# Low parts of weights made by adding loads, and more row pairs in seven products, in the last feed-forward layer of a decoder trunk

## The chip, the cores and the metric

One core of one Trainium2 chip. The metric is the device time of one execution in microseconds (us), taken as the median of several runs: 2597.03 us for the kernel before (3 runs, 2595.98 to 2597.09).

## What is computed

A trunk of two layers over 256 tokens of width 2048. Layer 0 mixes tokens by multi-scale retention, layer 1 by a short gated convolution; each is followed by a SwiGLU feed-forward of inner width 5632. Every sub-layer has an RMS norm, a shift, scale and gate from a conditioning vector, and a residual add. The change touches only the last feed-forward:

```python
def swiglu(h, w_in, w_out):
    a, b = jnp.split(h @ w_in, 2, axis=-1)
    return (jax.nn.silu(a) * b) @ w_out

# per layer i, after its mixer
h = (rms_norm(x, norm2_g[i]) * (1.0 + sc2) + sh2).astype(x.dtype)
x = (x + g2 * swiglu(h, ffn_w_in[i], ffn_w_out[i])).astype(x.dtype)
# at the end
return rms_norm(x, final_g).astype(x.dtype)
```

All is in float32.

## The kernel before, in words

**Products from high and low parts.** TensorE (PE) multiplies in a shortened float format (fp32r). To keep precision, every operand is split: hi is the value cast to fp32r, lo is the value minus hi. A product then takes three matmuls: hi by hi, hi by lo, lo by hi (`thrice`, lines 457 to 462; L461 is the one that reads the weights' low part).

**Where weights come from.** All weights but those of the modulation lie in one array `w_all` of 456 blocks of 128 x 2048 floats (1 MB), in the order of use. `fetch` (L370) loads a block into a `raw` buffer (three of them), by the queue of SyncE (SP). `prepare` (L376) turns it into pieces: for a plain block two halves of 1024 columns, pieces 0 and 1. For each, ScalarE (ACT) casts the half to `hi` (L402), and VectorE (DVE) subtracts to `lo` (L405). `hi` and `lo` have four buffers each (`PART_BUFS`), so piece n can be written only when PE has done with piece n - 4. `take` (L410) hands the parts of a piece to PE and, when it begins a piece, prepares on so that in the last stage three pieces lie ahead (`ahead_now`). PE's instructions stay in the order of the program; those of the other engines are ordered by a scheduler, close to the program's order.

**The last stage.** The last feed-forward holds tokens on the rows: 256 tokens are two halves of 128. Weights are taken in blocks of two rows (of 128) by two columns (of 512). Plain (`Group`), such a block takes 8 products of 128 x 128 by 128 x 512, that is 24 matmuls; each piece of 1024 columns serves 12. In sevens (`Seven`, L142; `sevens`, L1222) the same block takes 7 products by the Strassen-Winograd scheme, with sums and differences of the four weight parts and of the four token parts: 21 matmuls. For its weights `prepare` makes four pieces, 2 to 5: VectorE makes a difference of 1024 columns (L391) and two of 512 (L395, L397), and the pieces have 1024, 1024, 1024 and 512 columns. Pieces 2 to 4 serve 6 matmuls each and piece 5 serves 3. The token sums are made once for each row pair: for the input rows by `made_in_sums` before the first group, for output rows by `turned` (L1323) just after the two rows exist, both through `tokens_sums_of` (L1138). After the last block in sevens of a group, `mixed_sums` (L1235) combines four banks on VectorE.

The input projection runs in groups of eight row pairs (0 to 7), four groups in part 0 and six in part 1; before, pairs 3 and 5 go in sevens (`IN_SEVEN`). A group's result passes through SiLU and product, and is turned (eight transposes, L1329) during the next group, when that reaches its third row pair (`TURNS_AT`). The output projection runs after each part, in two groups of 1024 columns: ten row pairs in part 0, twelve in part 1, of which the three pairs 2, 4, 6 go in sevens (`OUT_SEVEN`). In the last output group the last three pairs are taken by single columns, for the tail. The grouped part of the last stage is the last 124 of the 456 blocks; 32 of them are in sevens before.

Of the kernel before, what the change touches and what calls it, by code (L numbers as in the profile page):

```python
# [10 lines left out]
F32 = mybir.dt.float32  # L11
F32R = mybir.dt.float32r
I32 = mybir.dt.int32
AF = mybir.ActivationFunctionType
ALU = mybir.AluOpType
PSUM = bass.MemoryType.PSUM

P = 128
# [14 lines left out]
HALF = 1024  # L33
# [4 lines left out]
LEAD = 6  # L38
ROOTS_AT, SPREAD_AT = 1, 3
TAIL_ROWS = 6  # L40
IN_SEVEN, OUT_SEVEN, TURNS_AT, BESIDE_CB, BESIDE_SUMS = (3, 5), (2, 4, 6), 2, 40, 48
LAST_TILES = 20, 24
STORE_AT, LOAD_AT = 0, 2
LEAD_RET, LEAD_CONV, LEAD_FFN = 6, 4, 2
# [97 lines left out]
class Seven:  # L142
# [6 lines left out]
    n = 2 * DV // P  # L149
# [12 lines left out]
def in_pairs(cols, rows, sevens):  # L162

    return [Seven(cols, r) if i in sevens else Group(cols, DV, ks=r) for i, r in rows]
# [13 lines left out]
def last_out(part):  # L178

    first, n = part * LAST_TILES[0], LAST_TILES[part]  # L180
    order = list(range(n // 2))
    if not part:
        a, b = order[-2:]
        order = order[:5] + [a, order[6], b, order[5], order[7]]
    rows = [(i, [first + 2 * i, first + 2 * i + 1]) for i in order]
    out = []
    for c in range(0, D, 2 * DV):
        cols, rest = [c, c + DV], 0
        if part and c + 2 * DV == D:
            rest = TAIL_ROWS // 2  # L190
        out.append(in_pairs(cols, rows[: len(rows) - rest], OUT_SEVEN))
        if rest:
            out[-1] += [Group([col], DV, ks=[k for _, r in rows[-rest:] for k in r]) for col in cols]
    return out
# [62 lines left out]
def trunk(ctx: ExitStack, tc: tile.TileContext, x_in, c_in, pos_in, w_mod, cols_in, gain_in, tab_in, w_all, out):  # L257
    nc = tc.nc
# [11 lines left out]
    def tmp(tag, shape=(P, S), dtype=F32, pool=work, bufs=None):  # L270
        return pool.tile(list(shape), dtype, tag=tag, name=name(tag), bufs=bufs)
# [11 lines left out]
    cols = const.tile([P, n_cols], F32, tag="cols", name="cols")  # L283
# [78 lines left out]
    in_seven, n = set(), 0  # L362
    for g in groups:
        if isinstance(g, Seven):
            in_seven.add(n // CHUNK)
        n += g.n * P * len(g.ks)

    pieces = [(i, p) for i in range(w_all.shape[0]) for p in ((2, 3, 4, 5) if i in in_seven else (0, 1))]

    def fetch():  # L370
        raw = wpool.tile([P, CHUNK], F32, tag="raw", name=name("raw"), bufs=RAW_BUFS)
# [4 lines left out]
    def prepare(between=None):  # L376
        if prepared[0] == len(pieces):
            return
        _, piece = pieces[prepared[0]]
        prepared[0] += 1  # L380
        if piece in (0, 2):
            if not fetched:
                fetch()
            raws[:] = [fetched.pop(0)]
            while first <= units[0] < early and len(fetched) < RAW_BUFS - 1 and n_fetched[0] < w_all.shape[0]:
                fetch()
        whole = raws[0]
        b = [whole[:, i : i + DV] for i in range(0, CHUNK, DV)]
        raw = whole[:, :HALF] if piece in (0, 4) else whole[:, HALF:]
        if piece == 2:  # L390
            nc.vector.tensor_tensor(differences, whole[:, DV : 3 * DV], whole[:, : 2 * DV], op=ALU.subtract)  # L391
        elif piece == 3:
            raw = differences
        elif piece == 4:
            nc.vector.tensor_tensor(b[1], b[2], differences[:, :DV], op=ALU.subtract)  # L395
        elif piece == 5:
            nc.vector.tensor_tensor(b[3], b[3], b[1], op=ALU.subtract)  # L397
            raw = b[3]
        width = raw.shape[1]
        hi = wpool.tile([P, HALF], F32R, tag="hi", name=name("hi"))[:, :width]  # L400
        lo = wpool.tile([P, HALF], F32R, tag="lo", name=name("lo"))[:, :width]
        nc.scalar.copy(hi, raw)  # L402
        if between:
            between()
        nc.vector.tensor_tensor(lo, raw, hi.bitcast(F32), op=ALU.subtract)  # L405
        ready.append((hi, lo, width))

    prepared, ahead_now = [0], [AHEAD]
# [270 lines left out]
    with ExitStack() as inner:  # L679
# [64 lines left out]
        with tc.tile_pool(name="start", bufs=1) as sp:  # L744
# [132 lines left out]
            due, step = [], [0.0]  # L877
# [245 lines left out]
    def turn(t, c):  # L1123
# [8 lines left out]
    needed(1, GT2)  # L1132
    in_cb = const.tile([P, D], F32R, tag="cb", name="in_cb")
    tokens_sums = [
        v.rearrange("p (i n) -> p i n", i=2) for v in (in_cb[:, : 6 * P], in_cb[:, 6 * P : 12 * P])
    ] + [mpool.tile([P, 2, 3 * P], F32R, tag="sums_of_tokens", name="sums_of_tokens")]

    def tokens_sums_of(a11, a21, a12, a22, third, others):  # L1138

# [11 lines left out]
    def parts(both):  # L1151

        return [both[:, i, t * P : (t + 1) * P] for i in range(2) for t in range(2)]

    in_sums = {}

    def made_in_sums():

        tmp("beside_sums", (P, BESIDE_SUMS), bufs=1)
        for i in IN_SEVEN:  # L1160
            both = tmp("u512", (P, 2, S), pool=mpool, bufs=3)
            for n in range(2):
                k = 2 * i + n
                high, low = [h[k].bitcast(F32)[:, v, :] for v in range(2)]
                nc.vector.tensor_tensor(both[:, n, :], high, low, op=ALU.add)
            tag = "low" if in_sums else "u"
            in_sums[i] = [tmp(tag, (P, 2, P), F32R, bufs=3) for _ in range(3)]
            tokens_sums_of(*parts(both), h[2 * i][:, :, P:], in_sums[i])

    def three(v):  # L1170
        return [v[:, :, n * P : (n + 1) * P] for n in range(3)]

    turns = [lambda t=t, c=c: turn(t, c) for c in range(4) for t in range(2)]

# [136 lines left out]
    def last_input(groups, pairs, seven):  # L1311

        ours, extra = gathered(groups, h, 0, in_sums)
        for (t, j), pt in ours.items():
            nc.vector.tensor_tensor(extra[t, j], pt, extra[t, j], op=ALU.add)
        ms = []
        for t in range(2):
            m = extra[t, 0]
            nc.scalar.activation(m, m, AF.Silu)
            nc.vector.tensor_tensor(m, m, extra[t, 1], op=ALU.mult)  # L1320
            ms.append(m)

        def turned():  # L1323
            for n, (dst, of) in enumerate(zip(pairs, seven)):
                pt = bank()
                for i in range(2):
                    for t, m in enumerate(ms):
                        c = slice((2 * n + i) * P, (2 * n + i + 1) * P)
                        nc.tensor.transpose(pt[:, i, t * P : (t + 1) * P], m[:, c], ident)  # L1329
                if of is not None:  # L1330
                    both = tmp("u512", (P, 2, S), pool=mpool, bufs=3)
                    nc.scalar.copy(both, pt)
                nc.scalar.copy(dst[:, :, 0, :], pt)
                nc.vector.tensor_tensor(dst[:, :, 1, :], pt, dst[:, :, 0, :].bitcast(F32), op=ALU.subtract)
                if of is not None:
                    tokens_sums_of(*parts(both), dst[:, 0, :, P:], [of])

        waiting.append(turned)

    def last_output(part, c, groups, act, base):  # L1340

        final = part and c

        def beside(i):
            if not part and not c and i == STORE_AT:
                gate_stored()
            if not part and not c and i == LOAD_AT:
                spread()
            if part and not c and i == LOAD_AT:
                last_gain = hpool.tile([P, D], F32, tag="h", name="last_gain")  # L1350
                nc.sync.dma_start(last_gain, gain_in.broadcast_to([P, D]))
                gain_of.extend(at(last_gain, v) for v in range(4))

        def mixed(extra):
            for (t, j), v in extra.items():
                gated(t, c + j, v, 0)

        sums = {i: three(v) for i, v in zip(OUT_SEVEN, tokens_sums)}
        ours, extra = gathered(groups, act, base, sums, beside, mixed if final else None)
        if final:  # L1360
            return
        for (t, j), pt in ours.items():
            nc.vector.tensor_tensor(extra[t, j], pt, extra[t, j], op=ALU.add)
        for (t, j), v in extra.items():
            gated(t, c + j, v, MOD_PRIO)
            if part:
                xs, n = at(xt[t], c + j), c + j
                nc.scalar.activation(v, xs, AF.Square, accum_out=total[:, t, n : n + 1])
                nc.vector.tensor_tensor(xs, xs, gain_of[n], op=ALU.mult)
# [16 lines left out]
    for part in range(2):  # L1386
        n = LAST_TILES[part] // 2
        mid = mids(LAST_TILES[part]) if part else first_mid
        if not part:
            first_rows(mid[-2:])  # L1390
            made_in_sums()
            ahead_now[0] = AHEAD + 1
        for i, groups in enumerate(LAST_IN[part]):
            seven = [tokens_sums[OUT_SEVEN.index(q)] if q in OUT_SEVEN else None for q in (2 * i, 2 * i + 1)]
            last_input(groups, mid[2 * i : 2 * i + 2], seven)
        act = [mid[k // 2][:, k % 2] for k in range(2 * n)]
        for c, groups in enumerate(LAST_OUT[part]):
            last_output(part, 2 * c, groups, act, part * LAST_TILES[0])
# [37 lines left out]
```

## Time and profile before

| | |
|---|---|
| median of 3 runs | 2597.03 us |
| profiled execution, its own time | 2600.71 us |
| its span, first to last instruction | 2598.8 us |
| granted TensorE clock, mean | 0.999 |
| read from memory | 685.08 MB, 264 GB/s over the span |
| raw loads of `w_all` | 456 of 1024 KB, median 4.9 us from issue to landing |
| weight subtractions on VectorE (L405) | 944, 1129.9 us |
| weight casts on ScalarE (L402) | 944, 973.1 us |

How to read it: PE is TensorE's matmuls, PEld its weight loads, POOL is GpSimd, SP is SyncE. "busy" is the time in which an engine had an instruction running; matmuls are pipelined, so that two that follow each other overlap in the rows. In groups of instructions, `out<-in` names what is written and read, `xcount` is how often, then come the busy time and the mean of one in ns, and behind the second bar the engine's idle time ahead of these instructions and what ended it. "DMA share" is the mean busy share of the core's 16 DMA engines.

### The profile page before, as it was taken

Reading aid. Unit: us, or ns where it says so; the run is one execution under the profiler, and the core shown is the slowest. Engines: PE = TensorE matmul, PEld = TensorE weight load, DVE = VectorE, ACT = ScalarE, POOL = GpSimd, SP = SyncE. Lnnn points to the kernel's source line nnn. Section 1 sums busy time; section 2 is a strip of 40 time slices with the busy share of each in tenths; the row PEclk is TensorE's granted clock in tenths of the full one; section 3 lists DMA queues with packets and bytes.
Section 4 is the critical chain, followed back from the end, with each engine's and each line's share of the span. In section 5 each row is a group of like instructions: output and inputs, shape, how many; then the busy total and the mean of one; then the engine's idle time right before and its main releaser. Section 6 shows DMA issues by size and latency. Waiting matters only on the chain.

```text
span 2598.8 us, 36365 instructions
## 1 busy us (share of the span) xinstructions
PE 2567.0 (99%) x14211; PEld 2241.0 (86%) x14211; DVE 2157.4 (83%) x2702; ACT 1289.4 (50%) x1768; POOL 125.7 (5%) x232
## 2 busy tenths in 40 slices
PE   7999999999999999999999999999999999999998
PEld 6898889888889888888888898888998888888886
DVE  7988978887698887777777889988988888888877
ACT  5544543444456454334444454444565554555554
POOL 0000000110000000100001001000000000000000
PEclk9999999999999999999999999999999999999999
DMA  9975668877676888787778868877845565554653
GB/s 399 387 290 221 255 246 300 299 261 276 244 284 247 330 325 305 298 299 302 294 284 296 299 237 313 326 290 277 305 171 204 190 217 203 184 207 182 221 200 146
DMA packets 96686, 689.55 MB, mean 265 GB/s; under 512 B 10737, under 2 KB 12161, under 8 KB 13441
## 3 DMA queue, kind: packets, MB, share of 16 engines
q1 hardware_dynamic: 96514, 687.23, 71.1%
q8 instruction: 111, 1.82, 0.3%
q14 instruction: 61, 0.50, 0.1%
HBM read 685.08 MB, written 2.11 MB: 264 GB/s over the span
## 4 chain that ended last, share of the span: by engine, by line
PE 84%; DVE 7%; DMA 5%; issue 2%; ACT 1%; ACTq 0%; POOLq 0%; POOL 0%; DVEq 0%; SPq 0%
PE bank L447 25%; PE bank L450 14%; PE bank L461 12%; PE bank L460 12%; PE bank L462 12%; DMA raw<-w_all 4%; DVE lo L405 3%; DMA raw<-w_mod 2%; PE bank L496 2%; PE bank L495 1%; PE bank L494 1%; PE bank L627 1%; PE bank L629 1%; PE bank L628 1%; DVE raw L755 1%
## 5 line engine op out<-in xcount | busy, mean ns | idle before, releaser
L402 ACT CAST hi<-raw 128x1024 fp32r<-128x1024 f32 (+1 forms) x944 | 973.1, 1039 | 1037.0 <-PE bank L462 385.6
L405 DVE TENSOR_TENSOR lo<-raw,hi 128x1024 fp32r<-128x1024 f32 (+1 forms) x944 | 1129.9, 1203 | 347.4 <-ACT hi L402 340.0
L447 PE MATMUL bank<-h,hi 128*128 128x512 f32 x2016 | 699.2, 390 | 0.0
L450 PE MATMUL bank<-h,lo 128*128 128x256 f32 x2016 | 568.4, 282 | 0.0
L447 PEld LDWEIGHTS bank<-h,hi 128*128 128x128 f32 x2016 | 378.3, 188 | 79.2
L460 PE MATMUL bank<-hi,h 128*128 128x512 f32 x1072 | 420.1, 392 | 1.8 <-DVE rm L739 1.8
L461 PE MATMUL bank<-lo,h 128*128 128x512 f32 x1072 | 418.3, 390 | 0.7 <-DVE lo L405 0.7
L462 PE MATMUL bank<-hi,h 128*128 128x512 f32 x1072 | 417.6, 390 | 0.0
L318 DVE SCALAR_TENSOR_TENSOR raw<-raw,cb 128x2048 f32<-128x2048 f32 x160 | 365.6, 2285 | 23.2 <-DMA raw<-w_mod 22.9
L450 PEld LDWEIGHTS bank<-h,lo 128*128 128x128 f32 x2016 | 381.0, 189 | 0.0
L447 PE MATMUL bank<-mid,hi 128*128 128x512 f32 x922 | 319.8, 390 | 0.0
L450 PE MATMUL bank<-mid,lo 128*128 128x256 f32 x922 | 260.1, 282 | 0.4 <-DVE lo L405 0.4
L462 PEld LDWEIGHTS bank<-hi,h 128*128 128x128 f32 x1072 | 201.4, 188 | 42.6
L460 PEld LDWEIGHTS bank<-hi,h 128*128 128x128 f32 x1072 | 201.8, 188 | 41.8 <-DVE rm L739 2.4
L461 PEld LDWEIGHTS bank<-lo,h 128*128 128x128 f32 x1072 | 201.9, 188 | 39.9 <-DVE lo L405 1.1
L447 PEld LDWEIGHTS bank<-mid,hi 128*128 128x128 f32 x922 | 173.0, 188 | 36.2
L450 PEld LDWEIGHTS bank<-mid,lo 128*128 128x128 f32 x922 | 174.3, 189 | 0.7 <-DVE lo L405 0.7
L447 PE MATMUL bank<-rm,hi 128*128 128x512 f32 x496 | 172.6, 390 | 0.0
L496 PE MATMUL bank<-h,lo 128*128 128x256 f32 x512 | 146.2, 286 | 5.2 <-DVE lo L405 5.2
L494 PE MATMUL bank<-h,hi 128*128 128x256 f32 x512 | 145.6, 284 | 3.2 <-ACT h L783 3.2
L495 PE MATMUL bank<-h,hi 128*128 128x256 f32 x512 | 145.6, 284 | 0.7 <-DVE h L784 0.7
L450 PE MATMUL bank<-rm,lo 128*128 128x256 f32 x496 | 139.9, 282 | 0.0
(248 smaller groups left out, 3092.4 us busy)
## 6 DMA issues: line engine op xcount, KB each, us to landing
raw<-w_all SPq DMA_DIRECT2D x456, 1024.0 KB, 4.9
raw<-w_mod SPq DMA_DIRECT2D x192, 1024.0 KB, 5.3
x<-x_in SPq DMA_DIRECT2D x4, 512.0 KB, 5.5
out<-xt SPq DMA_DIRECT2D x4, 512.0 KB, 3.0
decay<-tab_in SPq DMA_DIRECT2D x8, 128.0 KB, 2.7
x<-gate_row SPq DMA_DIRECT2D x2, 512.0 KB, 4.4
last_gain<-gain_in SPq DMA_DIRECT2D x1, 1024.0 KB, 4.6
cols<-cols_in SPq DMA_DIRECT2D x1, 152.0 KB, 8.5
```

Source lines behind the costliest of these rows:

```text
L318: nc.vector.scalar_tensor_tensor(raw, raw, 1.0, cb, op0=ALU.mult, op1=ALU.mult, accum_out=total)
L402: nc.scalar.copy(hi, raw)
L405: nc.vector.tensor_tensor(lo, raw, hi.bitcast(F32), op=ALU.subtract)
L447: nc.tensor.matmul(pt, hi, h, start=fresh and k == g.ks[0], stop=False, skip_group_check=True)
L450: nc.tensor.matmul(pt[:, 1, :], lo, h[:, 0, :], start=False, stop=last and k == g.ks[-1], skip_group_check=True)
L460: nc.tensor.matmul(o, hi, w_hi, start=first, stop=False)
L461: nc.tensor.matmul(o, hi, w_lo, start=False, stop=False)
L462: nc.tensor.matmul(o, lo, w_hi, start=False, stop=last)
L494: nc.tensor.matmul(pt, hi, h[:, 0, :], start=first, stop=False, skip_group_check=True)
L495: nc.tensor.matmul(pt, hi, h[:, 1, :], start=False, stop=False, skip_group_check=True)
L496: nc.tensor.matmul(pt, lo, h[:, 0, :], start=False, stop=last, skip_group_check=True)
L627: nc.tensor.matmul(pt, hi, high, start=k == 0, stop=False, skip_group_check=True)
```

## The change

Two things, both in the last stage.

First, more row pairs go in sevens: in the input groups 3, 4 and 6 instead of 3 and 5; in the output groups 2, 4, 5, 6 (part 0) and 2, 4, 6, 8 (part 1) instead of 2, 4, 6. Of the 124 blocks, 46 are then in sevens. The token sums of the added pairs get buffers made of spare parts of other tiles (`single_sums`).

Second, from the first grouped block of the last stage on, the low part of the second half of every plain block (piece 1) isn't subtracted on VectorE. ScalarE writes minus hi into `lo`, and a load issued by GpSimd brings the same 1024 columns from `w_all` once more and adds them onto `lo`.

```diff
-IN_SEVEN, OUT_SEVEN, TURNS_AT, BESIDE_CB, BESIDE_SUMS = (3, 5), (2, 4, 6), 2, 40, 48
+IN_SEVEN, OUT_SEVEN, TURNS_AT, BESIDE_CB, BESIDE_SUMS = (3, 4, 6), ((2, 4, 5, 6), (2, 4, 6, 8)), 2, 40, 48
...
-        out.append(in_pairs(cols, rows[: len(rows) - rest], OUT_SEVEN))
+        out.append(in_pairs(cols, rows[: len(rows) - rest], OUT_SEVEN[part]))
...
+    last_block = min(in_seven) - IN_SEVEN[0]
     pieces = [(i, p) for i in range(w_all.shape[0]) for p in ((2, 3, 4, 5) if i in in_seven else (0, 1))]
+
+    def low_by_dma(block, piece):
+
+        return piece == 1 and block >= last_block
...
-        _, piece = pieces[prepared[0]]
+        block, piece = pieces[prepared[0]]
...
-        nc.vector.tensor_tensor(lo, raw, hi.bitcast(F32), op=ALU.subtract)
+        if low_by_dma(block, piece):
+            nc.scalar.mul(lo, hi.bitcast(F32), -1.0)
+            nc.gpsimd.dma_start(lo, w_all[block, :, piece * HALF : (piece + 1) * HALF], accum_op=ALU.add)
+        else:
+            nc.vector.tensor_tensor(lo, raw, hi.bitcast(F32), op=ALU.subtract)
...
     tokens_sums = [
-        v.rearrange("p (i n) -> p i n", i=2) for v in (in_cb[:, : 6 * P], in_cb[:, 6 * P : 12 * P])
-    ] + [mpool.tile([P, 2, 3 * P], F32R, tag="sums_of_tokens", name="sums_of_tokens")]
+        [v.rearrange("p (i n) -> p i n", i=2)] for v in (in_cb[:, : 6 * P], in_cb[:, 6 * P : 12 * P])
+    ] + [[mpool.tile([P, 2, 3 * P], F32R, tag="sums_of_tokens", name="sums_of_tokens")]]
+    single_sums = [in_cb[:, n * P : (n + 2) * P].rearrange("p (i n) -> p i n", i=2) for n in (12, 14)]
...
         tmp("beside_sums", (P, BESIDE_SUMS), bufs=1)
+        for tag, n in (("u", 3), ("low", 3), ("sum", 4)):
+            single_sums.extend(tmp(tag, (P, 2, P), F32R, bufs=n) for _ in range(n))
...
-            tag = "low" if in_sums else "u"
-            in_sums[i] = [tmp(tag, (P, 2, P), F32R, bufs=3) for _ in range(3)]
+            in_sums[i] = [single_sums.pop() for _ in range(3)]
             tokens_sums_of(*parts(both), h[2 * i][:, :, P:], in_sums[i])
+        if single_sums[2:]:
+            tokens_sums.append([single_sums.pop() for _ in range(3)])
...
-        sums = {i: three(v) for i, v in zip(OUT_SEVEN, tokens_sums)}
+        sums = {i: three(v) for i, v in zip(OUT_SEVEN[part], tokens_sums)}
...
-            seven = [tokens_sums[OUT_SEVEN.index(q)] if q in OUT_SEVEN else None for q in (2 * i, 2 * i + 1)]
+            due = OUT_SEVEN[part]
+            seven = [tokens_sums[due.index(q)] if q in due else None for q in (2 * i, 2 * i + 1)]
```

More of the change, by code (lines that the diff above doesn't have):

```diff
@@ L1165, in made_in_sums @@
                 nc.vector.tensor_tensor(both[:, n, :], high, low, op=ALU.add)
-            tag = "low" if in_sums else "u"
-            in_sums[i] = [tmp(tag, (P, 2, P), F32R, bufs=3) for _ in range(3)]
+            in_sums[i] = [single_sums.pop() for _ in range(3)]
             tokens_sums_of(*parts(both), h[2 * i][:, :, P:], in_sums[i])
+        if single_sums[2:]:
+            tokens_sums.append([single_sums.pop() for _ in range(3)])
     def three(v):
-        return [v[:, :, n * P : (n + 1) * P] for n in range(3)]
+        return [v[0][:, :, n * P : (n + 1) * P] for n in range(3)] if len(v) == 1 else v
     turns = [lambda t=t, c=c: turn(t, c) for c in range(4) for t in range(2)]
@@ L1335, in turned @@
                 if of is not None:
-                    tokens_sums_of(*parts(both), dst[:, 0, :, P:], [of])
+                    tokens_sums_of(*parts(both), dst[:, 0, :, P:], of)
         waiting.append(turned)
```

## The prediction

> **What bounds the kernel now.** First the page's busy times, then the last stage alone (windows), where the whole change lies, then who waits there.
>
> ```profile
> span 2598.8 us, 36365 instructions
> PE 2567.0 (99%) x14211; PEld 2241.0 (86%) x14211; DVE 2157.4 (83%) x2702; ACT 1289.4 (50%) x1768; POOL 125.7 (5%) x232
> ```
> ```profile
> core 0: us, PE busy (x) PEld busy (x) DVE busy (x) ACT busy (x) POOL busy (x), PEclk, DMA share, GB/s
> 1920.00:2540.00 620.00, 619.46 (x2787) 513.67 (x2786) 515.91 (x610) 330.25 (x385) 0.00 (x0) 1.00 0.55 198
> 2113.00:2129.00 16.00, 15.46 (x68) 12.50 (x67) 15.21 (x16) 8.35 (x9) 0.00 (x0) 1.00 0.56 197
> 1780.00:1920.00 140.00, 138.88 (x916) 127.62 (x915) 123.16 (x183) 76.53 (x129) 4.56 (x11) 1.00 0.71 259
> ```
> ```profile
> ACT hi L402 <- PE bank L462: 253.0, 217, 2.0
> PE bank L461 <- DVE lo L405: 0.5, 1, 0.5
> ```
>
> From 1920 to 2540 us PE is idle 0.54 us of 620, all of it in the third row's window, at a granted clock of 1.00. So PE is the bound, and its own matmuls set the time. VectorE is at 83% (515.91 of 620), ScalarE at 53%, the DMA engines at 0.55, GpSimd at nothing. The waits (window 1940 to 2540) say how the supply is coupled: ScalarE waits for PE 217 times, because a piece's buffer comes free only when PE has finished the piece four before it. Weights are thus made at the latest moment the four buffers allow, and PE never notices. How much lead that is decides this case, so I read it off the order of time.
>
> The first fence below is ScalarE's timeline, the second PE's, around a block in sevens (its seven products end at 2320.33) and the plain blocks after it; the columns are start and duration.
>
> ```profile
> 2318.54 1.05 ACT L402 CAST hi<-raw 128x1024 fp32r<-128x1024 f32 x1 [0.32 <-PE bank L462]
> 2323.25 1.06 ACT L402 CAST hi<-raw 128x1024 fp32r<-128x1024 f32 x1 [1.27 <-PE bank L462]
> ```
> ```profile
> 2318.06 0.39 PE L462 MATMUL bank<-hi,h 128*128 128x512 f32 x1
> 2318.29 0.39 PE L460 MATMUL bank<-hi,h 128*128 128x512 f32 x1
> 2320.33 0.39 PE L460 MATMUL bank<-hi,h 128*128 128x512 f32 x1
> 2323.05 0.39 PE L460 MATMUL bank<-hi,h 128*128 128x512 f32 x1
> 2323.27 0.39 PE L461 MATMUL bank<-lo,h 128*128 128x512 f32 x1
> 2331.21 0.39 PE L460 MATMUL bank<-hi,h 128*128 128x512 f32 x1
> 2331.43 0.39 PE L461 MATMUL bank<-lo,h 128*128 128x512 f32 x1
> ```
>
> A matmul occupies PE for less than its 0.39 us: 2320.33 to 2323.05 holds the 12 of one plain piece, so 2.72/12 = 0.2267 us each. The buffer that the seven's second piece leaves at 2318.29 is refilled from 2318.54 for the **second half of the plain block behind it**, which PE starts at 2323.05 and whose low part it reads first at 2323.27. Only 4.76 us of matmuls lie between: half of a seven's products (1.36 + 0.68) and one plain piece (2.72). Among plain blocks a hi copy of 2323.25 serves a piece whose low part is read at 2331.43: 8.18 us.
>
> **Part 1: more sevens.** Input groups go from rows 3, 5 to 3, 4, 6 (10 groups, +10), output groups from three to four rows (2 groups in each of two parts, +4): 14 blocks with 7 products of 3 matmuls for 8. PE saves 14 x 3 x 0.2267 = **9.5 us**. On the path in full, since PE has no idle there.
>
> Their price on the other engines, from the groups of the window 1940 to 2540 (shapes kept apart; mean ns after the comma):
>
> ```profile
> L405 DVE TENSOR_TENSOR lo<-raw,hi 128x1024 fp32r<-128x1024 f32 x225 | 273.8, 1222 | 64.2 <-ACT hi L402 59.8
> L402 ACT CAST hi<-raw 128x1024 fp32r<-128x1024 f32 x225 | 236.0, 1055 | 206.5 <-PE bank L462 190.3 <-issue 6.2 <-DVE lo L405 5.0
> L391 DVE TENSOR_TENSOR x<-raw 128x1024 f32<-128x1024 f32 x29 | 35.4, 1219 | 2.8 <-DMA raw<-w_all 2.8
> L405 DVE TENSOR_TENSOR lo<-raw,hi 128x512 fp32r<-128x512 f32 x30 | 20.7, 691 | 18.0 <-ACT hi L402 17.7
> L395 DVE TENSOR_TENSOR raw<-raw,x 128x512 f32<-128x512 f32 x30 | 20.6, 687 | 0.3
> L397 DVE TENSOR_TENSOR raw<-raw 128x512 f32<-128x512 f32 x29 | 19.9, 687 | 0.3
> L402 ACT CAST hi<-raw 128x512 fp32r<-128x512 f32 x30 | 18.7, 623 | 47.5 <-PE bank L462 40.9 <-DVE lo L405 6.6
> ```
>
> A plain block costs VectorE 2 x 1.22 = 2.44 us; one in sevens 1.22 + 3 x 1.22 + 2 x 0.69 + 0.69 = 6.95, though PE spends only 4.76 on it. So 14 x 4.51 = 63 us more on VectorE, 14 x 1.68 = 24 more on ScalarE (3 x 1.055 + 0.623 for 2 x 1.055). Three more sums of tokens (one for the input rows, one in each output part) I cost by VectorE's timeline, seven operations of which these are a short and a long one:
>
> ```profile
> 2303.49 0.28 DVE L1145 TENSOR_TENSOR u<-u,u 128x128 f32<-128x128 f32 x1
> 2304.83 0.55 DVE L512 TENSOR_TENSOR in_cb<-u,in_cb 128x384 fp32r<-128x384 f32 x1
> ```
>
> About 2 us each, 6 in all.
>
> **Part 2: low parts by loads.** 124 blocks belong to the grouped part, 124 - 46 = 78 stay plain. For the second half of each, VectorE loses a subtraction: 78 x 1.22 = 95 us. On balance VectorE falls by 95 - 63 - 6 = 26 us. That buys nothing by itself, because PE hardly ever waited for it; it only lets the sevens in. Two sevens in a row (rows 3, 4) ask 13.9 us of VectorE in 9.5 of PE; the lead and the two subtractions saved in rows 1 and 2 cover most. The window 2113 to 2129, a seven right behind a sum of tokens, shows 0.54 us lost for one such crowding; bounds 0 to 1 us in the 10 input groups, and I take **+2 us**. If that cover is gone, PE waits for lo L405.
>
> In place of the subtraction stands a chain: hi copy on ScalarE, a negation on ScalarE (same shape, 1.055 us; 78 make 82 us, which its idle 47% holds), then a wait on GpSimd, a load issued there that adds 512 KB of weights onto the tile, and PE's wait for its landing. Behind GpSimd's waiting instruction stand only later loads and, at the very end, a few adds of totals, so its queue is no matter. Behind PE's waiting matmul stands everything. Behind the negation stand later hi copies, which wait for PE anyway. SP's raw loads go on, but share the 16 DMA engines; raw buffers come free a little earlier, with VectorE's second read gone.
>
> So the question is the time **L** from the end of the negation to the landing, against the lead left:
>
> - behind a seven: hi from 2318.54, negation done 2 x 1.05 later, 2320.64; first read 2323.27: **2.63 us**;
> - among plain blocks: 2323.25 + 2.11 = 2325.36 to 2331.43: **6.07 us**.
>
> A plain block stands directly behind a seven twice in each input group (rows 5, 7) and four times in each output group: 20 + 16 = **36** of the 78. A wait there doesn't help the next such place, whose buffer comes free after it. Of the other 42, about 16 have no other wait within their lead; a wait lengthens the lead of the next.
>
> The trace has no load by GpSimd and none that adds. The nearest rows are SP's (size, median us to landing), and GpSimd's own operations. The first row is of the window 1940 to 2540, the next four of the whole run:
>
> ```profile
> raw<-w_all SPq DMA_DIRECT2D x112, 1024.0 KB, 4.8
> ```
> ```profile
> raw<-w_mod SPq DMA_DIRECT2D x192, 1024.0 KB, 5.3
> out<-xt SPq DMA_DIRECT2D x4, 512.0 KB, 3.0
> decay<-tab_in SPq DMA_DIRECT2D x8, 128.0 KB, 2.7
> x<-gate_row SPq DMA_DIRECT2D x2, 512.0 KB, 4.4
> ```
> ```profile
> L323 POOL TENSOR_SCALAR mcol<-msum,cols 128x1 f32<-128x1 f32 x48 | 41.4, 863 | 423.4 <-DVE raw L318 423.2
> ```
>
> Below, L is hardly under 2.7 us: a quarter of the bytes, and no add, takes that. Above, a load that is served after a whole raw load takes 4.8 + 4.8 = 9.6. I take the 1 MB load as nearest, since an add must fetch the weights and the tile, 2 x 512 KB. In the stretch of w_mod, at a DMA share of 0.71, that took 5.3 us; here the share rises from 0.55 (124 raw loads of 1 MB and 78 adds that move as much, over a longer stretch: 0.55 x 202/124 x 620/740 = 0.75). GpSimd's issue I put at one of its operations, 0.86. An estimate: **L = 6.2 us**. Then PE waits 36 x (6.2 - 2.63) = **128.5 us** behind sevens and 16 x 0.13 = **2 us** elsewhere.
>
> The Trainium skill, DMA: Bandwidth & Descriptors, section Anatomy of one DMA — SWDGE (gpsimd) path, gives a GpSimd DMA 2.0 us plus its bytes over 436e3, for 512 KB an estimate of 3.2 us. By that rule the waits are 36 x 0.57 = 21 us and the time about 2610; it speaks for less harm than my row, and no run here shows it yet.
>
> **Sum**, against the profiled execution: 2600.7 - 9.5 + 128.5 + 2 + 2 = 2723.7 (its span 2598.8 lies 1.9 inside; it is 3.7 above the median of the runs). Against the median of 2597.0: **2720 us**.
>
> **Rivals.** Each is a landing time.
>
> 1. *Late* (forecast): L from 4.5 to 7, 36 x 1.87 = 67 to 36 x 4.37 = 157 us, plus 16 x 0.93 = 15 at the upper end: about 2657 to 2762.
> 2. *Quick, but not quick enough*: the add costs no second fetch and L is like the 512 KB rows, 3.0 to 4.4, or a little under. 36 x 0.27 = 10 (at 2.9) to 36 x 1.77 = 64: 2599 to 2653. For it: those rows. Against it: one is a store, the other was issued by SP, and neither adds. The skill's rule above falls here.
> 3. *Hidden*, the other side: L under 2.63, or the pieces get a longer lead than the before trace shows. Only the 9.5 us, less 2, remain: 2589. It turns at 36 x (L - 2.63) = 7.5, that is L = 2.84. For it: 128 KB in 2.7 us, and DMA engines that are 45% idle. Against it: four times the bytes.
> 4. *Queued*: the adds go at less than a copy's pace, or behind raw loads, L from 7 to 9.6; 36 x 4.37 to 6.97, plus 16 x 0.93 to 3.53: 2762 to 2897. For it: one raw load of the last 60 us is waited for 7.43 us even now. Past that, raw loads themselves come late.
>
> ```profile
> 2541.13 7.43 DMA raw<-w_all
> ```
>
> **Numbers.** Chances: 0.54 for 1, 0.18 for 2, 0.10 for 3, 0.18 for 4. Likeliest 2720. Range 2610 to 2850 (L from about 3.2 to 8.7): left out are 3 (0.10), the quickest of 2 (0.04) and the latest of 4 (0.05). A measurement of this kernel tells about 0.2%, 5.2 us, from no change. Faster 0.10 (rival 3); within 0.2% 0.04 (rival 2 with L near 2.9); slower 0.86.
>
> **What would show it.** In the profile of after: 14 x 3 = 42 fewer 512-wide matmuls; 78 negations of 1.05 us on ScalarE and 78 loads on GpSimd's queue; VectorE's busy time down by some 26 us, with 1.22 us subtractions gone from second halves; DMA share up to about 0.75. PE's waits name the adding load at L461, 36 of them about 3.6 us long, at rows 5 and 7 of each input group, and few elsewhere. The issue-to-landing row of the new loads is L itself, less GpSimd's step. I am wrong if PE is still without idle from 1920 on (rival 3), if the waits stand evenly at all 78 (rival 4), or if they name lo L405 (VectorE) or raw.

## The result, and the profile after

The changed kernel takes 2873.87 us (median of 4 runs, 2871.80 to 2877.27) against 2597.06 before: a ratio of 1.1067, 95% interval 1.1048 to 1.1086. It is slower, as forecast, but by 277 us where 123 were forecast, and it lies above the stated range (2610 to 2850).

First the page of after: span, busy times, the queue of the new loads, and their landing time.

```profile
span 2870.2 us, 36747 instructions
...
PE 2652.9 (92%) x14169; PEld 2285.1 (80%) x14169; DVE 2139.7 (75%) x2720; ACT 1388.3 (48%) x1888; POOL 193.7 (7%) x310
...
q0 software_dynamic: 11232, 40.90, 7.7%
...
raw<-w_all SPq DMA_DIRECT2D x456, 1024.0 KB, 5.0
...
lo<-w_all POOLq DMA_DIRECT2D x78, 512.0 KB, 7.0
```

The counts came as forecast: 42 matmuls fewer (14211 to 14169), 78 loads. VectorE is 18 us less busy. But PE is **busier by 85.9 us with fewer matmuls**, and its idle time grew as well. So there are two losses, to be kept apart: the span grew by 271.4 us; PE's idle time went from 2598.8 - 2567.0 = 31.8 to 2870.2 - 2652.9 = 217.3, that is 185.5 more; the other 85.9 are busy time, or 95.4 beyond what PE should have saved.

The last stage as one window, then the waits of PE there (line numbers are those of after: L407 the hi cast, L411 the negation, L412 the adding load, L469 to L471 the three matmuls, L470 the first reader of the low part):

```profile
1920.00:2870.00 950.00, 752.43 (x2953) 594.75 (x2952) 543.97 (x685) 456.05 (x540) 72.14 (x86) 0.89 0.62 182
```
```profile
PE bank L470 <- DMA lo<-w_all: 187.1, 51, 7.0
```

All but 0.7 us of PE's waits name the adding load. And the granted clock in this stretch is 0.89 where it was 1.00 (the column behind POOL's). PE's timeline shows how the two belong together; here is the plain block behind the two sevens of rows 3 and 4 of an input group:

```profile
2530.57 0.39 PE L469 MATMUL bank<-hi,h 128*128 128x512 f32 x1
2537.17 0.80 PE L470 MATMUL bank<-lo,h 128*128 128x512 f32 x1 [6.21 <-DMA lo<-w_all]
2537.76 0.63 PE L471 MATMUL bank<-hi,h 128*128 128x512 f32 x1
2538.19 0.63 PE L469 MATMUL bank<-hi,h 128*128 128x512 f32 x1
...
2541.17 0.58 PE L470 MATMUL bank<-lo,h 128*128 128x512 f32 x1
2541.59 0.39 PE L471 MATMUL bank<-hi,h 128*128 128x512 f32 x1
2541.82 0.39 PE L469 MATMUL bank<-hi,u 128*128 128x512 f32 x1
```

After a wait of 6.21 us the matmuls start 0.427 us apart (2537.76, 2538.19) instead of 0.227, for ten matmuls, then the old pace is back. A short wait in the same kernel has no such tail:

```profile
1992.52 0.50 PE L470 MATMUL bank<-lo,h 128*128 128x512 f32 x1 [1.86 <-DMA lo<-w_all]
1992.86 0.40 PE L471 MATMUL bank<-hi,h 128*128 128x512 f32 x1
1993.09 0.40 PE L469 MATMUL bank<-hi,h 128*128 128x512 f32 x1
```

Over all of PE's timeline of that stage there are 50 waits over 0.3 us, 188 us together. Of the 37 that last 3.38 us or more, every one is followed by 6 to 14 matmuls at half the pace; of the 13 that last 2.88 us or less, none. 36 of the 50 stand behind a block in sevens, where the prediction put them: 168 us, 4.7 us each on average. The other 14 make 20 us.

The Trainium skill, TensorE: Matmul & The Clock Gate, Part 1 (on the HAM clock gate), says that TensorE's clock is halved after an idle window of about 3.4 us and comes back after a busy one. This trace agrees in the pace (0.427 for 0.227 us) and in a window of that length. It does not take a wholly idle window, though: what it takes is measured under **Hi matmuls first**.

Where one such landing comes from, first ScalarE's timeline, then GpSimd's:

```profile
2525.78 1.06 ACT L407 CAST hi<-raw 128x1024 fp32r<-128x1024 f32 x1 [0.26 <-PE bank L471]
2526.87 1.06 ACT L411 ACTIVATE lo<-hi 128x1024 fp32r<-128x1024 f32 x1
```
```profile
2528.23 0.87 POOL L412 DMA_DIRECT2D lo<-w_all  x1 [18.78 <-ACT lo L411]
```

hi and the negation are made at once, 1.06 us each, as forecast; GpSimd's issue takes 0.87 (0.86 was assumed). Then the load lands 8.9 us after its issue began, and PE goes on at 2537.17.

### The profile page after: what moved, and what is told of

Its sections match the earlier page's. It is cut to its first block, busy times and chain, and to the rows that moved or that the text cites. A ratio compares the mean times of both kernels' runs of the same rounds, so it can differ in the third digit from the quotient of the medians.

```text
span 2870.2 us, 36747 instructions
## 1 busy us (share of the span) xinstructions
PE 2652.9 (92%) x14169; PEld 2285.1 (80%) x14169; DVE 2139.7 (75%) x2720; ACT 1388.3 (48%) x1888; POOL 193.7 (7%) x310
## 4 chain that ended last, share of the span: by engine, by line
PE 76%; DMA 15%; DVE 3%; issue 3%; ACT 3%; POOLq 0%; ACTq 0%; POOL 0%; DVEq 0%; SPq 0%
PE bank L456 26%; PE bank L459 14%; DMA lo<-w_all 12%; PE bank L470 9%; PE bank L471 8%; PE bank L469 8%; PE bank L505 2%; PE bank L504 2%; PE bank L503 2%; DMA raw<-w_all 2%; ACT hi L407 2%; DVE lo L414 1%; PE bank L636 1%; PE bank L638 1%; PE bank L637 1%
## 5 line engine op out<-in xcount | busy, mean ns | idle before, releaser
L407 ACT CAST hi<-raw 128x1024 fp32r<-128x1024 f32 (+1 forms) x958 | 979.0, 1030 | 1142.5 <-PE bank L471 514.5
L414 DVE TENSOR_TENSOR lo<-raw,hi 128x1024 fp32r<-128x1024 f32 (+1 forms) x880 | 1046.4, 1195 | 560.7 <-ACT hi L407 559.1
L470 PE MATMUL bank<-lo,h 128*128 128x512 f32 x1032 | 425.7, 412 | 107.3 <-DMA lo<-w_all 106.5
L469 PE MATMUL bank<-hi,h 128*128 128x512 f32 x1032 | 418.8, 406 | 1.2 <-DVE rm L748 1.2
L471 PE MATMUL bank<-hi,h 128*128 128x512 f32 x1032 | 418.7, 406 | 0.0
L470 PEld LDWEIGHTS bank<-lo,h 128*128 128x128 f32 x1032 | 204.4, 198 | 164.6 <-DMA lo<-w_all 120.4
L471 PEld LDWEIGHTS bank<-hi,h 128*128 128x128 f32 x1032 | 204.3, 198 | 42.9
L469 PEld LDWEIGHTS bank<-hi,h 128*128 128x128 f32 x1032 | 203.2, 197 | 43.6 <-DVE rm L748 1.8
L470 PE MATMUL bank<-lo,mid 128*128 128x512 f32 x288 | 129.3, 449 | 81.6 <-DMA lo<-w_all 81.6
```

The source lines that it names most:

```text
L469: nc.tensor.matmul(o, hi, w_hi, start=first, stop=False)
L470: nc.tensor.matmul(o, hi, w_lo, start=False, stop=False)
L471: nc.tensor.matmul(o, lo, w_hi, start=False, stop=last)
```

## Experiments

Three theories were set against each other. The **theory**: the whole loss is PE waiting for the landing of the adding loads, at places with a short lead, plus the half clock that a long wait brings. **Rival one**: the slow matmuls come from the loads' traffic, not from idleness. **Rival two**: the added sevens, or the hand-over to GpSimd as such, make the loss. A further question was what the landing time is made of. Kernels with an interval were executed several times; the others are one execution.

The bookkeeping, from each kernel's page: "idle" is span minus PE busy, less the 31.8 us of before; "slow" is PE's busy time beyond 2567.0, corrected for matmuls saved (9.5 us) or added. "Landing" is the median of the adding loads, from the start of GpSimd's instruction on.

| kernel | us | idle | slow | landing |
|---|---|---|---|---|
| the change | 2873.9 | 185.5 | 95.4 | 7.0 |
| sevens only | 2593.6 | 0.5 | 2.8 | - |
| loads only | 2872.4 | 183.5 | 88.3 | 7.3 |
| loads only far from sevens | 2699.7 | 68.6 | 35.3 | 9.0 |
| filler matmuls in the waits | 2834.8 | 77.3 | 39.4 | 7.5 |
| loads that don't add | 2801.5 | 128.8 | 81.5 | 5.6 |
| hi matmuls first | 2804.3 | 129.7 | 83.4 | 7.2 |
| no raw loads beside | 2767.0 | 117.6 | 58.3 | 5.5 |
| GpSimd subtracts | 2626.0 | 25.4 | 11.5 | - |
| sevens only, hi matmuls first | 2591.7 | 0.7 | 0.1 | - |

Not all of "slow" is slow pace. In the changed kernel's last stage, matmuls that start more than 0.33 us apart make 69 us of its 95, and the first ones behind a wait 13. About 9 belong to the waits: the last matmul ahead of a wait counts with its whole 0.39 us, where it otherwise takes 0.227. The few us left are not assigned.

**Sevens only.** All low parts on VectorE again.

```diff
-        return piece == 1 and block >= last_block
+        return False
```

> Part 1 alone: 46 blocks in sevens, every low part subtracted on VectorE as before. Theory (the loss is made by waits for the landing of the adding loads, and by the half clock after them): no such waits, so near 2597 - 9.5, plus what VectorE cannot keep up with. An input group then asks about 5 x 2.44 + 3 x 6.95 = 33 us of weights and some 10 us of other work of VectorE in 42.4 us of matmuls, so waits of 0 to 3 us in each of 10 groups: 2588 to 2618, and PE waits for lo of VectorE. Rival (the sevens themselves, by VectorE's load, make the loss): above 2650.

2593.58 us; ratio to before 0.9978, interval 0.9969 to 0.9988: **0.2% faster than before**. Its busy times on the page, the window of the last stage that the prediction used, and PE's waits for VectorE from 1940 us to the end:

```profile
PE 2560.3 (99%) x14169; PEld 2234.4 (86%) x14169; DVE 2215.5 (85%) x2798; ACT 1313.7 (51%) x1810; POOL 133.3 (5%) x232
```
```profile
1920.00:2540.00 620.00, 619.53 (x2778) 511.28 (x2777) 576.50 (x708) 357.92 (x430) 1.17 (x1) 1.00 0.54 201
```
```profile
PE bank L470 <- DVE lo L414: 1.8, 3, 1.3
```

VectorE carries 58 us more than before, 93% of that window (576.5 of 620) for 83%, and PE is busy in 619.5 of it, as before. So the sevens aren't the cause, and the loads that were to make room for them weren't needed.

**Loads only.** Part 2 alone, with `IN_SEVEN` and `OUT_SEVEN` as before.

```diff
-IN_SEVEN, OUT_SEVEN, ... = (3, 4, 6), ((2, 4, 5, 6), (2, 4, 6, 8)), 2, 40, 48
+IN_SEVEN, OUT_SEVEN, ... = (3, 5), ((2, 4, 6), (2, 4, 6)), 2, 40, 48
```

> Part 2 alone: the row pairs in sevens as before (32 blocks), the low part of the second half of all 92 plain blocks by the adding load. Theory: PE gets no matmul back, 32 blocks stand directly behind a seven and wait as in the changed kernel, 165/36 = 4.6 us each and about 2.3 us of half clock, and some 20 us of shorter waits: 2597 + 32 x 6.9 + 20 = about 2840. Rival (the loss comes from both parts together, such as VectorE's load by the added sevens): below 2750.

2872.42 us, the changed kernel's time, and 32 us above the expectation: 92 loads instead of 78, with 66 waits over 0.3 us where the changed kernel has 50. The 34 outside the places behind sevens make 38 us, not 20, and "slow" is 88 us, not the 74 of 32 x 2.3. The loads alone make the loss.

**Loads only far from sevens.**

```diff
-        return piece == 1 and block >= last_block
+        return piece == 1 and block >= last_block and block - 1 not in in_seven
```

> As the changed kernel, but a plain block directly behind a block in sevens gets its low part from VectorE again: 42 loads stay, 36 go. Theory: the 36 long waits and all of the half clock go. Left are waits of landing time minus 6.07 us where two plain blocks follow each other: by the 7.2 us of the changed kernel about 1.1 us at some 20 places, too short for the half clock: 2597 - 9.5 + 22 + 0 to 15 of VectorE = 2610 to 2625. Rival (the loads slow PE by their traffic wherever they run): above 2700, half of the loss.

2699.67 us; ratio 1.0386 (1.0370 to 1.0402). A miss for the number, which stands where the rival begins. The 36 waits did go, but 13 new ones of 3.5 to 7.1 us came, one in each input group and three in output groups, with a half-clock tail each. Away from these 13 tails no matmul of the stage runs at half the pace, though 42 loads run: their traffic delays the landings, it doesn't slow PE. The loads landed later than in any other kernel:

```profile
lo<-w_all POOLq DMA_DIRECT2D x42, 512.0 KB, 9.0
```

One such load, and in the same stretch VectorE waiting for a raw load:

```profile
2487.82 10.89 DMA lo<-w_all
```
```profile
2495.31 1.23 DVE L396 TENSOR_TENSOR x<-raw 128x1024 f32<-128x1024 f32 x1 [2.21 <-DMA raw<-w_all]
```

The lead is nearly as I gave it: here the negation ends at 2487.53, 11.2 us ahead of the landing, and PE waits 5.4 of them, which leaves 5.8 for 6.07. But L isn't a constant. Of the 42 loads, the 8 with no raw load in flight beside them landed in 6.6 us (median), the 15 beside two in 9.2, the 7 beside three in 11.1. A load that is longer in flight also meets more raw loads, so this alone doesn't show which way it goes; the run without raw loads below does.

**Filler.** 16 matmuls by a tile of zeros ahead of the low part's first read, at 35 of the 36 places behind sevens.

```diff
+FILL = 16
...
+    zero = mpool.tile([P, 8], F32R, tag="zero", name="zero")
+    nc.scalar.mul(zero, ident[:, :8], 0.0)
+    zero = zero[:, :1].to_broadcast([P, P])
...
+                    weights = take(g, k, *item)
+                    if k == g.ks[1] and not j and i and isinstance(groups[i - 1], Seven):
+                        for _ in range(FILL):
+                            nc.tensor.matmul(ours[0, 0], zero, weights[0], start=False, stop=False)
-                    by_token([ours[t, j] for t in range(2)], *take(g, k, *item), act[k - base], *ends)
+                    by_token([ours[t, j] for t in range(2)], *weights, act[k - base], *ends)
```

> As the changed kernel, with 16 matmuls more, of zeros by the high part, ahead of the first read of the low part at 35 of the 36 places behind a block in sevens (3.6 us in a wait of about 4.6; they add nothing to the result). Theory (PE's half clock follows from its idleness): the landings end as before, the waits shrink to about 1 us, and the 9 to 14 matmuls at half rate behind each go: 2874 - 35 x 2.3 = about 2793. Rival (the slow matmuls come from the loads' traffic or from power): the slow matmuls stay, 2874 or more.

2834.77 us: **faster with 560 more matmuls** (127 us of them). The last filler matmuls, the wait, and what follows it, in PE's timeline (L471 reads the low part here):

```profile
2529.81 2.24 PE L1328 MATMUL bank<-hi,zero 128*128 128x512 f32 x9
2531.89 0.39 PE L470 MATMUL bank<-hi,h 128*128 128x512 f32 x1
2533.02 0.50 PE L471 MATMUL bank<-lo,h 128*128 128x512 f32 x1 [0.73 <-DMA lo<-w_all]
2533.36 0.39 PE L472 MATMUL bank<-hi,h 128*128 128x512 f32 x1
2533.59 0.40 PE L470 MATMUL bank<-hi,h 128*128 128x512 f32 x1
```
```profile
1920.00:2833.00 913.00, 823.08 (x3504) 655.21 (x3502) 543.49 (x685) 456.82 (x537) 72.27 (x86) 0.98 0.65 188
```

The pace behind the wait is whole, the stretch's clock is 0.98 again for 0.89, and "slow" fell from 95 to 39, with all 78 loads and their traffic in place. That settles rival one: the half clock follows PE's idleness. The time came out 42 us above the expectation because the loads landed half a microsecond later (7.5), some waits were shorter than the filler that went into them, and 9 waits, of 1.95 to 5.05 us, still have a long tail.

**Loads that don't add.**

```diff
-            nc.gpsimd.dma_start(lo, w_all[...], accum_op=ALU.add)
+            nc.gpsimd.dma_start(lo, w_all[...])
```

> As the changed kernel, but GpSimd's load writes the weights over the tile instead of adding them (the low parts of these 78 halves are then left out of the computation and replaced by the weights themselves). Theory (the add costs a second fetch, of the tile): landing about 1.5 us sooner, 5.7 us instead of 7.2, waits of about 3.1 us at 36 places, half clock behind some: 2700 to 2760. Rival (the time is that of GpSimd's path, add or not): landing and time unchanged, 2860 to 2880.

2801.51 us. The page's rows of the loads and of their queue:

```profile
lo<-w_all POOLq DMA_DIRECT2D x78, 512.0 KB, 5.6
...
q0 software_dynamic: 11232, 40.90, 4.4%
```

The add costs 1.4 us of a landing (7.0 to 5.6), close to the theory's 1.5. About 0.3 of it is GpSimd's own instruction, 0.54 us for 0.87. With the same packets and bytes on record, the queue takes 4.4% of the DMA engines' span for 7.7%, so the engines are longer at an add; that the rest is a second fetch of the tile is not shown. The time is above the expected 2700 to 2760, since most of the waits of 2.6 to 4 us that remain keep the half clock ("slow" 81.5).

**No raw loads beside.**

```diff
+    ring = [None] * RAW_BUFS
...
+        if n_fetched[0] < last_block + 3:
+            raw = wpool.tile(...)
+            nc.sync.dma_start(raw, w_all[n_fetched[0]])
+            ring[n_fetched[0] % RAW_BUFS] = raw
+        raw = ring[n_fetched[0] % RAW_BUFS]
```

> As the changed kernel, but the raw loads of the last stage are left out after its first three blocks (the blocks then work on old weights; the adding loads stay). It shows the landing without raw loads beside it. Theory (the adding load shares the DMA engines with raw loads of 1 MB, and that is the part of the landing that varies): landing falls from 7.0 to about 4.5 to 5, the waits behind sevens to 2 to 2.5 us, no half clock: 2660 to 2700. Rival (GpSimd's path and the add alone take the time): landing 6.5 to 7, time above 2820.

2767.04 us; the page's row:

```profile
lo<-w_all POOLq DMA_DIRECT2D x78, 512.0 KB, 5.5
```

The landing lies between theory and rival: 1.5 us of the 7.0 is the raw loads' company, and 5.5 is there without it. The time misses the theory's 2660 to 2700: the waits behind sevens are 3.2 us on average, and "slow" is still 58 us. The shortest of the 78 landings is 5.3 us, so no arrangement of raw loads would bring one under the 2.63 us of lead. No run leaves out both the add and the raw loads; if their 1.4 and 1.5 us add up, some 4.1 of the 7.0 would remain, an estimate, and what makes them stays open.

**Hi matmuls first.** The changed kernel with one more edit: in every plain half the eight matmuls by hi, then the four by lo; nothing else.

```diff
-                for j, item in enumerate(g.items):
...
+                for o, (a, b), (w_hi, _) in row:
+                    nc.tensor.matmul(o, a, w_hi, start=ends[0], stop=False)
+                    nc.tensor.matmul(o, b, w_hi, start=False, stop=False)
+                for o, (a, _), (_, w_lo) in row:
+                    nc.tensor.matmul(o, a, w_lo, start=False, stop=ends[1])
```

> As the changed kernel, but in every plain half PE does the eight matmuls by the high part first and the four by the low part after them: the first read of the low part comes 7 matmuls later, 1.6 us more lead, with the same matmuls. Theory: each of the 36 waits of about 4.6 us shrinks to about 3.0, and the half clock goes where a wait falls under 3 us, so 36 x 1.6 = 57 and some 40 to 60 us of the clock: 2755 to 2780. Rival (PE's order makes no difference, the landing moves with it): 2850 or more.

2804.33 us. That misses the expected 2755 to 2780. Idle fell by 56 us (57 expected): lead is worth its full length. But "slow" fell by 12 only (83 for 95), where 40 to 60 were expected: here waits from 1.85 us on were followed by slow matmuls, though not all. The limit near 3 us that the changed kernel shows isn't a fixed one.

What decides can be read from the granted clock. In every trace here it changes only on a fixed grid of 3.41 us. First the changed kernel, three windows of that grid around the wait of 6.21 us shown above; then, in this run, a wait of 2.60 us that ends at 2661.77 and has a tail; then, in the run with loads that don't add, a wait of 3.69 us that ends at 2222.91 and has none (behind the width stand PE's busy time and, behind POOL's, the clock):

```profile
2531.32:2534.73 3.41, 0.00 (x0) 0.00 (x0) 1.75 (x2) 0.49 (x1) 0.00 (x0) 1.00 0.95 265
2534.74:2538.15 3.41, 0.98 (x2) 0.84 (x3) 0.00 (x0) 0.00 (x0) 0.00 (x0) 0.50 0.34 66
...
2541.57:2544.97 3.40, 3.40 (x16) 2.80 (x15) 1.12 (x2) 1.82 (x3) 0.00 (x0) 1.00 0.16 19
```
```profile
2657.72:2661.13 3.41, 1.45 (x7) 0.88 (x5) 3.33 (x4) 0.62 (x1) 0.00 (x0) 1.00 0.92 195
2661.14:2664.55 3.41, 2.78 (x7) 2.20 (x8) 0.61 (x2) 0.00 (x0) 0.00 (x0) 0.50 0.02 5
```
```profile
2217.70:2221.10 3.40, 1.51 (x7) 0.94 (x5) 2.40 (x4) 2.99 (x4) 0.54 (x1) 1.00 0.94 345
2221.11:2224.51 3.40, 1.60 (x7) 1.34 (x8) 1.56 (x2) 0.00 (x0) 0.00 (x0) 1.00 0.94 278
```

The shorter wait leaves PE idle for 1.96 us of one window; the longer is cut by the grid into 1.89 and 1.80. Over the last stage of all eleven traces, 2310 windows at full clock, PE's idle time in a window decides almost alone: under 1.85 us none was followed by a window at half clock, over 1.95 all were. A window at half clock was followed by another when PE was idle for 0.60 us of it or more, and by a full one at 0.54 or less. So a wait's length alone does not decide; where it falls on the grid does too.

**GpSimd subtracts.** No negation, no load.

```diff
-            nc.scalar.mul(lo, hi.bitcast(F32), -1.0)
-            nc.gpsimd.dma_start(lo, w_all[...], accum_op=ALU.add)
+            nc.gpsimd.tensor_tensor(lo, raw, hi.bitcast(F32), op=ALU.subtract)
```

> As the changed kernel, but GpSimd itself subtracts hi from raw for these 78 halves: no negation, no load, no landing. Theory (what costs is the landing, not that the work leaves VectorE): the lead behind a seven is then 2.63 + 1.06 = 3.7 us from the end of hi; if GpSimd needs 2 to 3 us for 128x1024, PE hardly waits: 2588 to 2600. If it needs 5 us, 36 waits of 1.3 us: about 2635, without the half clock. Rival (any hand-over to GpSimd makes the loss): 2800 or more.

2625.95 us; ratio 1.0107 (1.0090 to 1.0124). One such subtraction takes:

```profile
L411 POOL TENSOR_TENSOR lo<-raw,hi 128x1024 fp32r<-128x1024 f32 x78 | 222.6, 2861 | 486.5 <-ACT hi L407 477.1 <-issue 7.8 <-DMA raw<-w_all 1.7
```

A tenth of the loss, for the same halves taken from VectorE. It misses the 2588 to 2600 that the expectation gives for 2 to 3 us a subtraction, and most of what PE waits for is VectorE's low parts:

```profile
PE bank L469 <- DVE lo L413: 20.1, 12, 3.4
PE bank L469 <- POOL lo L411: 6.6, 2, 3.3
```

VectorE's own subtractions got longer where GpSimd's ran beside them, as the last section says. So the hand-over to GpSimd isn't what costs 277 us (rival two); the landing is. It isn't free either.

**Sevens only, hi matmuls first.** The two edits above, joined.

> Part 1 alone (no adding loads), with the eight matmuls by the high part ahead of the four by the low part in every plain half. Theory: with sevens alone PE waits 1.28 us in the last stage, so a longer lead for low parts has next to nothing to win: 2592 to 2595, the ratio that of the sevens alone. Rival (small waits for VectorE that the trace of sevens alone does not show are left): 2588 to 2590.

2591.74 us, ratio 0.9975 (0.9966 to 0.9985): the fastest here, but not told apart from the sevens alone (0.9969 to 0.9988).

## Why the prediction was wrong

By its own steps:

- **What bounds the kernel, and where**: right. PE was the bound, the four buffers set the lead, and the 36 places behind sevens take the long waits. Rival 3 (hidden) did not come, nor did waits on VectorE beyond 0.7 us, or on raw. Behind sevens L is 7.3 us on average, just past the forecast's own band (to 7), where rival 4 begins; the sums give 2777 for waits of 168 and 20 us. That the measured time lies well inside rival 4's range (2762 to 2897) is luck for it: the waits do not stand evenly at all 78 places, which was its sign, and the rest of the time has another reason. The DMA share is 0.62 in the stage, not 0.75, since the stage got longer.
- **Part 1, 9.5 us**: right in kind. The sevens alone give 5.3 us, with hi matmuls first 6.3 (medians, each against the kernel before on its chip). About 3 to 4 of the 9.5 are missing, and where they go stays open.
- **VectorE, +2 us**: nothing like it was seen; with sevens alone PE's idle grew by 0.5 us. The argument that the sevens needed part 2's room was also the change's own premise, and I took it over ("it only lets the sevens in"). The trace said 83% of the stage; 93% is still enough.
- **L = 6.2 us**: too small. The waits behind sevens are 168 us instead of 128.5, the 14 others 20 instead of 2. The terms that I added (an add fetches twice, raw loads run beside it, GpSimd's issue) each have a measured counterpart, 1.4, 1.5 and 0.87 us, the last one partly inside the first; but the path without an add and beside raw loads is already 5.6, above the 4.8 of an SP load of twice the size. The row from issue to landing isn't L less GpSimd's step, as the prediction reads it: it holds that step and leaves out 0.3 us from the end of the negation to the issue. The Trainium skill's estimate of 3.2 us, from DMA: Bandwidth & Descriptors, section Anatomy of one DMA — SWDGE (gpsimd) path, fits no landing here; the shortest of any run is 3.8, without the add.
- **Two rows read wrongly**: the 7.43 us of the raw load under rival 4 are the time from its issue to its landing, not a wait; VectorE waited 2.3 us for it. And 5.3 us is the landing of `w_mod` over the whole run; in the window with a DMA share of 0.71 it was 5.7. Neither changes the step below.
- **The step that failed**: "Then PE waits 36 x (6.2 - 2.63) = 128.5 us". Its wait was mis-sized by the L above, and it took the wait for the whole cost. Behind each long wait PE ran at half its clock for about ten matmuls, for which the sum has no term: 95 us of busy time, of which about 80 are slow pace. Between the sum against the profiled execution, 2723.7, and the time of after's profiled execution, 2872.1, lie 148 us: 95 are PE's busy time, and 53 are idle time beyond the 132.5 that the sum has (185.5 measured). Either alone would have stayed inside the range. The last stage before could not show the half clock, since PE waited less than 1 us at a time there; but the clock column was there to ask "what if it does".

## What to carry to other kernels

A wait put into a gapless stream of matmuls can cost more than its length: where it left PE idle for some 1.9 us of a 3.41 us window, about ten matmuls at half pace came on top, some 2 us here. Price that as well as the wait. Before moving work off a busy engine, check that it is late at all: here VectorE at 93% of a stage cost PE nothing. An offload through memory has to fit the shortest lead in the order of the work, not the mean one, at its landing time beside the traffic that is there anyway: here 2.63 us of lead against landings of 5.3 us and more.

## What the hardware showed that I had not expected

- A load by GpSimd of 512 KB lands in 5.6 us beside raw loads, without an add; SP's raw loads of 1 MB in the same kernel need 4.9 (medians, from the issue on).
- The granted clock follows PE's idle time in windows of 3.41 us on a fixed grid. A wait of 2.60 us halved it and one of 3.69 did not.
- GpSimd's subtraction of 128x1024 takes 2.86 us on average, with single ones up to 7.9 us, and VectorE's of that size went up to 3.4 us there: the 65 with a GpSimd subtraction beside them took 1.63 us (median), the 150 others none above 1.23. The Trainium skill, SBUF — State Buffer, section Who interferes with whom, says that a VectorE instruction with two SBUF inputs contends with a GpSimd one that reads SBUF; the trace agrees.
- PE got faster by doing useless work: 127 us of matmuls by zeros made the kernel 39 us shorter.
